# The squared-ReLU MLP of layer 0 as seven products of halves, with the modulation and bias rows between its steps

## The chip, the cores and the metric

The program runs on one core of a Trainium2 chip. The core has five engines that matter here: PE (TensorE, matrix products), DVE (VectorE), ACT (ScalarE), POOL (GpSimd) and SP (SyncE, which here issues most DMAs). Each takes its instructions in order; between engines semaphores order the work. The metric is the device time of one launch in microseconds (us).

## The reference

Two encoder layers on x of 1024 rows and 1024 columns, in float32. Layer 0 mixes with latent attention (`mla_mixer`), layer 1 with dilated window attention (`dilated_mixer`). The change is in the last line, and in where `mod` is computed:

```python
for i in range(2):
    mod = (silu(c) @ ada_w[i] + ada_b[i]).reshape(B, 6, 1024)
    shift1, scale1, gate1, shift2, scale2, gate2 = (mod[:, s, None, :] for s in range(6))
    h = rms_norm(x, norm_mix[i]) * (1 + scale1) + shift1
    x = x + gate1 * (mla_mixer if i == 0 else dilated_mixer)(h, ...)
    h = rms_norm(x, norm_mlp[i]) * (1 + scale2) + shift2
    x = x + gate2 * (square(relu(h @ mlp_w1[i])) @ mlp_w2[i])      # 1024 -> 4096 -> 1024
```

## The kernel before

**Products.** Every float32 product is made of three: `split` writes an operand as a high part (ACT) and a low part (DVE's subtraction, line 117, or another engine's through `lo_eng`), and `mm3` (lines 387 to 389) does high × high, high × low and low × high into PSUM. A matmul here is 128x128 by 512 columns unless said otherwise.

**Layer 0's MLP** is `mlp` (line 919 on). It walks 16 chunks `c` of 256 hidden columns. `up` multiplies the weights of a chunk with h, transposed (`psu`, 48 matmuls a chunk and half of the rows), applies Relu on ACT, the square on DVE, and splits; `down` multiplies that with the chunk's 256 rows of `mlp_w2` (`psy`) and DVE adds the result to x in SBUF (`x<-x,psy`, line 960). All of x stays in SBUF.

**Fillers.** Between its steps `mlp` calls functions from the list `filler`: `ada_step`, `bias_even` once, and `write`. `ada_step` works off the modulation row of the coming layer: each call issues the load of the next 512 KB piece of `ada_w` (tile `adaw`, on SP, in program order) and does the sum of the piece loaded by the call before on DVE (`ada_sum`, line 171, tile `adacc`); after eight pieces `ada_end` adds the bias row and lets a few small matmuls (`psac`) sum over the partitions. `bias_even` builds the position bias tables of layer 1's attention, and each `write` sends a piece of them to DRAM (tile `bt` reads them later). The modulation rows of both layers are worked off in one list: (0, 2), (0, 4), (0, 3), (0, 5), then (1, 1), (1, 0), (1, 2), (1, 4), (1, 3), (1, 5), where the second number is s above. Three of the calls are made by layer 0's `proj_res`.

**Layer 1's MLP** is `mlp7` (line 1003 on), which computes both products as a two-by-two block product with seven block products in place of eight. In the up half each of 16 pairs of 128 hidden columns takes seven products `(L.., R..)` in the order of the list `order`, where L11, L12, L22, S1 to S4 are sums of quarters of the weights (`ws` by POOL, split into `wf`), and R11, R21, R22, T1 to T4 are sums of quarters of h, split once into `hf` by `h_forms`. One product is 12 matmuls (`psm<-hf,wf`). The results are summed, put through Relu and square (`square`), summed again (`u_sums`, tiles `us`) and stored to DRAM (`uf`, `u_store`). The down half goes product by product, each in eight steps `gr` of 24 matmuls (`psm<-dh,dl`): `d_load`, called two steps ahead, loads the u form (`ufr`) and the needed quarters of `mlp_w2` (`w2r`, up to three), `d_form`, one step ahead, makes the weight's form (`w2s`, `w2T`) and splits both; T2's step also keeps the forms of T3 and T2 in SBUF. At the end of a product its four PSUM tiles are combined, multiplied with the gate, added to a part of x (`fin`; x is loaded again from DRAM, `xm`) and stored. What is the same in both layers' tails is `h_steps`, which makes h for the next stage.

**Output projection.** `proj_res` multiplies the attention's result with `w_o`, adds to x, and runs the steps that make h between its products. With `forms=True` (layer 1) these are `h_forms`, and x is stored to `xm` by POOL's DMA queue.

**What sets the order.** The program is written in an order; a planner that estimates the duration of every instruction may move them within an engine's queue, but what is `pinned` keeps its place: all DMAs of `ada_step` and `write`. Tiles come from pools with a fixed number of buffers: `G` (29 large tiles), `T` (temporaries, four a tag), and `X` (the auxiliary pool, `aux(n)`), and a load waits until the buffer that it takes is free.

Of the kernel before, what the change touches and what calls it, by code (L numbers as in the profile page):

```python
# [41 lines left out]
class K:  # L42
# [11 lines left out]
    def aux(self, n=16, ada=True):  # L54
# [3 lines left out]
        if ada:  # L58
            self.dap = self.ax.enter_context(self.tc.tile_pool(name=self.nm("ada"), bufs=2, reuse_waits="tile"))
# [149 lines left out]
    def ada_end(self, l, s, acc, row, psp, tag):  # L209

        nc = self.nc
        PS = lambda: psp.tile([P, 512], F32, tag=tag, bufs={"m": 1, "t": 3, "h": 2}.get(tag), name=self.nm("psac"))
# [12 lines left out]
    def ada_step(self, psp, tag):  # L225
# [3 lines left out]
        if self.ada_todo:  # L229
            l, s, j = self.ada_todo.pop(0)  # L230
            w = None
            if j < 8 or s % 3 == 2:
                w = self.dap.tile([P, 1024], F32, tag="w", name=self.nm("adaw"))
# [8 lines left out]
        if cur:  # L242
            l, s, j, w = cur
            if j == 0:
                self.ada_acc = self.dap.tile([P, 1024], F32, tag="acc", bufs=1, name=self.nm("adacc"))
# [42 lines left out]
    def xT(self, xh, d, psp, tag):  # L288

        ps = psp.tile([P, 512], F32, tag=tag, bufs={"h": 2, "u": 3, "m": 8}.get(tag), name=self.nm("pst"))  # L290
        for i in range(4):
            self.nc.tensor.transpose(ps[:, i * P : (i + 1) * P], xh[i][:, d * P : (d + 1) * P], self.ident)
        return ps
# [38 lines left out]
    def h_forms(self, xs0, xs1, mods, xalloc):  # L332
# [4 lines left out]
        R, keep = {}, []  # L337
# [16 lines left out]

        def first(psp, tag, d):
# [7 lines left out]
        def second(psp, tag, d):  # L363
            x1, x2 = (self.xT(xh[1], e, psp, tag) for e in (d, d + 4))
            t1, t4 = keep[d // 2][:, d % 2, :], keep[2 + d // 2][:, d % 2, :]
            r, t2 = xalloc("hs", (P, 2, 512), F32), self.T("ht2")
            t3, r22 = r[:, 0], r[:, 1]
            tt = lambda eng, o, x, y: eng.tensor_tensor(o, x, y, op=ALU.subtract)
# [13 lines left out]
        steps[1] += [lambda psp, tag, d=d: second(psp, tag, d) for d in range(4)]  # L382
        return (R, steps[0]), (R, steps[1])
# [483 lines left out]
    def proj_res(self, O, order, wo, gate, xs, mods, xalloc, ada, forms=False, done=None):  # L867
# [4 lines left out]
        with self.tc.tile_pool(name="psO", bufs=6, space=PSUM, reuse_waits="tile") as psp:  # L872
# [18 lines left out]
            if forms:  # L891
                (at, steps), (at1, steps1) = self.h_forms(xs[0:4], xs[4:8], mods, xalloc)
            else:
                at, steps = self.h_steps(xs[0:4], mods, xalloc, single=True)
                at1, steps1 = self.h_steps(xs[4:8], mods, xalloc, single=True)
            for i in range(8 + 6):
                if i < ada:
                    self.ada_step(psp, "h")
# [3 lines left out]
                if i >= 6:  # L902
                    part(pss[i - 6], *items[i - 6], 6, 8)
                    finish(pss[i - 6], *items[i - 6])
                    if items[i - 6][1] == 1:
                        steps.pop(0)(psp, "h")
                        if done:
                            done(items[i - 6][0])
            for i, (t, b) in enumerate(items):
# [3 lines left out]
                if b == 1:  # L913
                    steps1.pop(0)(psp, "h")
                    if done:
                        done(t + 4)
# [5 lines left out]
    def mlp(self, l, at0, second, gate, xs, filler, done, nxt=None):  # L922


        nc, a = self.nc, self.a
        NC = FF // 256
        with self.tc.tile_pool(name="psM", bufs=2, space=PSUM, reuse_waits="tile") as psp:

            def w1(c):
                return [self.wsplit(a["mlp_w1"][l, g * 512 : (g + 1) * 512, c * 256 : (c + 1) * 256]  # L930
                                    .rearrange("(d p) f -> p d f", p=P), (P, 4, 256), "w1") for g in range(2)]

            def w2(c):
                return [self.wsplit(a["mlp_w2"][l, (2 * c + f) * P : (2 * c + f + 1) * P, :], (P, 1024), "w2", row=gate)
                        for f in range(2)]

            def up(w, us, half, f):
                if f == len(us):
                    us.append([self.X(f"u{k}") for k in range(2)])
# [1040 lines left out]
```

## Time and profile before

| | |
|---|---|
| median of 3 runs | 3572.96 us (3566.36 to 3573.47) |
| profiled execution | 3570.81 us, span 3569.0 us, granted clock 0.983 |
| output projection, layer 0 | 741 to 835 us |
| MLP of layer 0 | 836.0 (first `psu`) to 1575.2 (last `psy`) |
| first matmul of layer 1's attention | 1580.3 |
| output projection, layer 1 | 2830 to 2922 |
| MLP of layer 1, up half | 2922.3 (first `psm`) to 3255.7 |
| MLP of layer 1, down half | 3256.9 to 3563.2 (last `psm`) |

Times of the stages are microseconds from the start of the span of the profiled execution. In the rows of the profile, `out<-in` names tiles without their numbers, `xN` counts instructions, a bracket or the part behind the last bar tells how long the engine sat idle before them and what ended that. PE and PEld are the matmuls and the weight loads of TensorE, PEclk is the clock that was granted to it as a share of full speed.

### The profile page before, as it was taken

How to read it: one execution, taken by the hardware profiler on the slowest of the kernel's cores; microseconds unless marked ns; L12 is line 12 of the kernel's file. 1: busy time of each engine (PE TensorE's matmuls, PEld its weight loads, DVE VectorE, ACT ScalarE, POOL GpSimd, SP SyncE). 2: the span in 40 equal slices, each digit the busy share in tenths (PEclk: the TensorE clock that was granted, in tenths of full speed). 3: DMA queues.
4: the chain of work that ended last, by engine and by line, in shares of the span. 5: the costliest groups of instructions: out<-in, count | busy, mean ns of one | idle time of the engine just before them, and what ended most of it. 6: DMA issues, size and time to landing. Idle time of an engine off the chain costs nothing.

```text
span 3569.0 us, 58220 instructions
## 1 busy us (share of the span) xinstructions
PE 3405.2 (95%) x21734; PEld 3036.5 (85%) x21734; DVE 2420.1 (68%) x4536; ACT 1573.2 (44%) x3279; POOL 1142.0 (32%) x1503
## 2 busy tenths in 40 slices
PE   6989989999999999999999999999999798999999
PEld 6878878878777888889999999999999676888887
DVE  6777877857555654566666666675787659776667
ACT  5557767633111222235555555564555334333432
POOL 6454444420011111112222222232333317653144
PEclk9999999999999999999999999999999898999999
DMA  5442222332444431123233333332333723446765
GB/s 183 136 160 71 101 68 69 113 118 90 106 106 107 112 95 48 60 91 93 80 107 107 103 100 103 98 88 68 107 104 99 192 86 121 157 151 240 275 227 165
DMA packets 341355, 419.99 MB, mean 118 GB/s; under 512 B 28901, under 2 KB 254482, under 8 KB 341066
## 3 DMA queue, kind: packets, MB, share of 16 engines
q1 hardware_dynamic: 331946, 394.11, 35.7%
q0 software_dynamic: 9120, 22.09, 1.9%
q8 instruction: 174, 2.85, 0.3%
q14 instruction: 115, 0.94, 0.1%
HBM read 319.35 MB, written 85.24 MB: 113 GB/s over the span
## 4 chain that ended last, share of the span: by engine, by line
PE 82%; DVE 6%; ACT 3%; DMA 3%; issue 2%; POOL 2%; SPq 0%; DVEq 0%; POOLq 0%; ACTq 0%
PE psproj L387 8%; PE psproj L389 8%; PE psproj L388 8%; PE psm L388 5%; PE psm L389 5%; PE psm L387 5%; PE psy L387 5%; PE psy L389 4%; PE psy L388 4%; PE psu L387 3%; PE psu L389 3%; PE psu L388 3%; PE pav L808 2%; PE pss L1590 2%; DMA adaw<-in_ada_w 2%
## 5 line engine op out<-in xcount | busy, mean ns | idle before, releaser
L404 POOL TENSOR_TENSOR w2r<-w2r,gate 128x1024 f32<-128x1024 f32 x32 | 84.7, 2648 | 677.4 <-DMA w2r<-in_mlp_w 664.1
L387 PE MATMUL psproj<-wqkh,hTp 128*128 128x256 f32 x1024 | 296.8, 290 | 0.0
L389 PE MATMUL psproj<-wqkh,hTp 128*128 128x256 f32 x1024 | 291.5, 285 | 0.0
L388 PE MATMUL psproj<-wqkl,hTp 128*128 128x256 f32 x1024 | 289.9, 283 | 0.0
L960 DVE TENSOR_TENSOR x<-x,psy 128x1024 f32<-128x1024 f32 x128 | 155.6, 1217 | 143.4 <-PE psy L389 143.4
L784 POOL TENSOR_SCALAR p<-p,arl 128x1024 f32<-128x1024 f32 x128 | 144.1, 1126 | 267.7 <-DVE arl L783 215.6
L1544 POOL TENSOR_TENSOR qn<-qn,dgain 128x128 f32<-128x128 f32 x192 | 90.1, 491 | 403.7 <-DVE qn L1541 373.9
L387 PE MATMUL psy<-w2h,u 128*128 128x512 f32 x512 | 203.1, 397 | 12.9 <-DVE x L960 12.9
L388 PE MATMUL psy<-w2l,u 128*128 128x512 f32 x512 | 202.0, 395 | 0.0
L389 PE MATMUL psy<-w2h,u 128*128 128x512 f32 x512 | 201.7, 394 | 0.0
L387 PE MATMUL psu<-hT,w1h 128*128 128x512 f32 x512 | 200.1, 391 | 0.9 <-DVE ht L315 0.9
L389 PE MATMUL psu<-hT,w1l 128*128 128x512 f32 x512 | 199.4, 390 | 0.0
L388 PE MATMUL psu<-hT,w1h 128*128 128x512 f32 x512 | 199.3, 389 | 0.0
L388 PEld LDWEIGHTS psproj<-wqkl,hTp 128*128 128x128 f32 x1024 | 195.8, 191 | 0.0
L389 PEld LDWEIGHTS psproj<-wqkh,hTp 128*128 128x128 f32 x1024 | 195.6, 191 | 0.0
L387 PEld LDWEIGHTS psproj<-wqkh,hTp 128*128 128x128 f32 x1024 | 195.6, 191 | 0.0
L1601 ACT ACTIVATE pd<-pd,dnb 128x192 f32<-128x192 f32 (+2 forms) x384 | 168.5, 443 | 54.8 <-DVE dnb L1599 54.6
L387 PE MATMUL psm<-hf,wf 128*128 128x512 f32 x448 | 177.1, 398 | 10.7 <-ACT wf L116 10.7
L389 PE MATMUL psm<-hf,wf 128*128 128x512 f32 x448 | 177.5, 397 | 5.6 <-DVE wf L117 5.6
L388 PE MATMUL psm<-hf,wf 128*128 128x512 f32 x448 | 177.7, 397 | 1.8 <-DVE hf L117 1.7
L1619 DVE TENSOR_TENSOR pT<-pspt,pT 128x512 f16<-128x512 f32 (+1 forms) x192 | 114.6, 598 | 94.8 <-ACT pT L1618 94.6
L117 DVE TENSOR_TENSOR pT<-ppt,pT 128x512 fp32r<-128x512 f32 x256 | 167.2, 681 | 14.1 <-ACT pT L116 13.3
(383 smaller groups left out, 11146.4 us busy)
## 6 DMA issues: line engine op xcount, KB each, us to landing
w2r<-in_mlp_w SPq DMA_DIRECT2D x104, 512.0 KB, 5.3
adaw<-in_ada_w SPq DMA_DIRECT2D x96, 512.0 KB, 5.8
w1r<-in_mlp_w SPq DMA_DIRECT2D x64, 512.0 KB, 4.1
bt<-bias SPq DMA_DIRECT2D x128, 256.0 KB, 3.2
ufr<-uf SPq DMA_DIRECT2D x56, 512.0 KB, 3.6
wqkr<-in_dil_w_in SPq DMA_DIRECT2D x96, 256.0 KB, 4.2
qkv<-st SPq DMA_DIRECT2D x32, 512.0 KB, 2.9
hraw<-qkv SPq DMA_DIRECT2D x32, 512.0 KB, 4.8
```

What stands on the lines that cost most here:

```text
L117: (lo_eng or nc.vector).tensor_tensor(lo, src, hi.bitcast(F32), op=ALU.subtract)
L387: mm(out, lh, rh, start=first, stop=False)
L388: mm(out, lh, rl, start=False, stop=False)
L389: mm(out, ll, rh, start=False, stop=last)
L404: nc.gpsimd.tensor_tensor(raw, raw, row, op=ALU.mult)
L784: nc.gpsimd.tensor_scalar(p, p, rl, 1.0, op0=ALU.mult, op1=ALU.mult)
L808: nc.tensor.matmul(ps[:, j % 2, :], heads[h]["v"][:, kt, :], u["pT"][hl][kt // 4][:, kt % 4, :], start=kt == 0 and hl == 0, stop=kt == 7 a ...
L960: nc.vector.tensor_tensor(xs[t], xs[t], ps, op=ALU.add)
L1544: nc.gpsimd.tensor_tensor(qq[:, i], qq[:, i], gain[:, g : g + 1, :].broadcast_to([P, 2, 64]), op=ALU.mult)
L1590: nc.tensor.matmul(ps[:, e * 256 : (e + 1) * 256], q[:, e, k, :], u["k"][:, e, w0 : w0 + 256], start=k == 0, stop=k == 1)
L1601: nc.scalar.activation(p[:, e, lo:hi], p[:, e, lo:hi], AF.Exp, bias=nb[:, e : e + 1], accum_out=stat[g][:, t, 1, 2 * pr + e : 2 * pr + e + 1])
L1619: nc.vector.tensor_tensor(pT[:, 1, 0 : 2 * n * P], ps[:, 0 : 2 * n * P], pT[:, 0, 0 : 2 * n * P], op=ALU.subtract)
```

## The change

`mlp` is gone; `mlp7` now serves both layers. What else is different:

- **Layer 0's output projection** runs `h_forms`, stores x to `xm[0]`, and makes no `ada_step`.
- **`h_forms`**: the four steps `second` make the sums and only the form T2; the forms of T3, T1, T4 and R22 are made afterwards, one kind a step (`others`). R22's low half moves from POOL to DVE.
- **Order of the seven**: up half R11, T2, R21, T3, T1, T4, R22 with the weights' forms made for pairs 0 and 1 together at the start; down half R11, T2, R21, T1, R22, T3, T4. The up half keeps its order; in the down half T1 and R22 come before T3 and T4, so the last part of x to be finished is that of rows 512 to 1023, columns 0 to 511.
- **Squares**: Relu and Square both on ACT (before: the square, or both, on POOL or DVE). `u_sums` uses one tile less.
- **In layer 0** the low half of the u forms for R11, R21, R22 and T3 is made by POOL (`lo_eng`); `ada_step` is called once a pair for pairs 2 to 14 (at k = 4) and, from the list `more`, in the steps 0 to 7 and from 16 on of the down half; `bias_even` is in step 1, a `write` in every second step from 6. The last product of the down half is interleaved with the first half of `h_steps` of layer 1. x goes to `xd` through POOL's queue, except the last four stores, which go through SP's.
- **Modulation row (1, 5)** moves to layer 1: one `ada_step` in each of the first 11 steps of its down half.
- **Pools**: `aux` has 19 buffers in layer 0 (16, beside a pool of three for `ada_step`) and 20 in layer 1, and `ada_step` takes its tiles from it.

```diff
         def second(psp, tag, d):
...
             tt(nc.vector, t1, t3, t1)
             tt(nc.vector, t2, r22, t1)
             form("T2", d, t2)
             tt(nc.gpsimd, t3, r22, t3)
-            form("T3", d, t3)
             tt(nc.gpsimd, t4, t4, t2)
-            form("T1", d, t1)
-            form("T4", d, t4)
-            form("R22", d, r22, nc.gpsimd)
+
+        def others(name):
+            src = {"T3": [r[0] for r in rs], "T1": keep[0:2], "T4": keep[2:4], "R22": [r[1] for r in rs]}[name]
+            for d in range(4):
+                form(name, d, src[d // 2][:, d % 2, :])
 
         steps[0] += [lambda psp, tag, d=d: first(psp, tag, d) for d in range(8)]
...
-            if forms:
-                (at, steps), (at1, steps1) = self.h_forms(xs[0:4], xs[4:8], mods, xalloc)
-            else:
-                at, steps = self.h_steps(xs[0:4], mods, xalloc, single=True)
-                at1, steps1 = self.h_steps(xs[4:8], mods, xalloc, single=True)
+            (at, steps), (at1, steps1) = self.h_forms(xs[0:4], xs[4:8], mods, xalloc)
             for i in range(8 + 6):
-                if i < ada:
-                    self.ada_step(psp, "h")
...
-        UF = {n: i for i, n in enumerate(("L11", "L12", "L22", "S1", "S2", "S3", "S4"))}
-
-        order = [("L11", "R11"), ("S2", "T2"), ("L12", "R21"), ("S3", "T3"), ("S1", "T1"), ("L22", "T4"), ("S4", "R22")]
+        UF = {n: i for i, n in enumerate(("L11", "S1", "L12", "L22", "S3", "S2", "S4"))}
+
+        prod = [("L11", "R11"), ("L12", "R21"), ("S4", "R22"), ("L22", "T4"), ("S1", "T1"), ("S2", "T2"), ("S3", "T3")]
+        order, order2 = ([prod[i - 1] for i in o] for o in ((1, 6, 2, 7, 5, 4, 3), (1, 6, 2, 5, 3, 7, 4)))
...
-                def square(eng, o, x, y):
+                def square(o, x, y):
 
                     tt(nc.vector, o, x, y)
-                    if eng is nc.vector:
-                        eng.scalar_tensor_tensor(o, o, 0.0, o, op0=ALU.max, op1=ALU.mult)
-                    else:
-                        nc.scalar.activation(o, o, AF.Relu)
-                        tt(eng, o, o, o, ALU.mult)
+                    nc.scalar.activation(o, o, AF.Relu)
+                    nc.scalar.activation(o, o, AF.Square)
...
             def u_sums(u):
-                u.s = [self.X("us", (P, 2, 512), F32) for _ in range(2)]
-                tt(nc.vector, u.s[0][:, 0], u.a[:, 1], u.b[:, 1])
-                tt(nc.vector, u.s[0][:, 1], u.s[0][:, 0], u.a[:, 0], ALU.subtract)
-                tt(nc.gpsimd, u.s[1][:, 0], u.a[:, 0], u.a[:, 1], ALU.subtract)
-                tt(nc.gpsimd, u.s[1][:, 1], u.b[:, 0], u.s[0][:, 1], ALU.subtract)
+                u.s, u.s4 = self.X("us", (P, 2, 512), F32), self.T("us4")
+                (u11, u12), (u21, u22), (s3, s2) = ((x[:, 0], x[:, 1]) for x in (u.a, u.b, u.s))
+                tt(nc.gpsimd, s3, u11, u12, ALU.subtract)
+                tt(nc.vector, u12, u12, u22)
+                tt(nc.vector, s2, u12, u11, ALU.subtract)
+                tt(nc.gpsimd, u.s4, u21, s2, ALU.subtract)
...
-                    self.split(hi, lo, x)
+                    self.split(hi, lo, x, lo_eng if x is u and rn in ("R11", "R21", "R22", "T3") else None)
...
+            for c in range(2):
+                quarters(c)
+            for n in ("L11", "L12"):
+                for c in range(2):
+                    u_forms(c, (n,))
+            for f in ((0, 0), (1, 0), None, (0, 2), None, (1, 2), None, None):
+                if f:
+                    up(us[f[0]], f[1])
+                else:
+                    steps.pop(0)(psp, "m")
+            for c in range(2):
+                sums(c)
+                u_forms(c, ("S2",))
+            todo = (1, 3, 4, 5, 6)
+            for j, i in enumerate(todo):
+                up(us[0], i)
+                if steps:
+                    steps.pop(0)(psp, "m")
+                if j < 4:
+                    for c in range(2):
+                        u_forms(c, (names[todo[j + 1]],))
+                up(us[1], i)
+                if j == 1:
+                    raws[2] = w_load(2)
+                elif j == 2:
+                    quarters(2)
+                    u_forms(2, names[0:1])
+                elif j == 3:
+                    sums(2)
+                    u_forms(2, names[1:3])
+                elif j == 4:
+                    raws[3] = w_load(3)
+                    u_forms(2, names[3:7])
             ld, fm = {}, {}
             dsteps = [(i, g) for i in range(7) for g in range(NP // 2)]
-            for c in range(NP):
-                todo = [1, 3, 4, 5, 6] if c < 2 else list(range(7))
-                if c == 0:
-                    u_forms(0, ("S3",))
...
+            for c in range(2, NP):
+                for k in range(7):
+                    if c == 2 and k in (0, 2):
+                        (u_sums(us[0]) if k == 0 else u_store(us[0], 0))
...
+                        u_sums(us[c - 1])
+                    elif k == 3:
+                        u_store(us[c - 1], c - 1)
+                    elif k == 4 and l == 0 and c + 1 < NP:
+                        self.ada_step(psp, "m")
+                    up(us[c], k)
...
+            more = list(more)
+            h = None
             c1, c2 = slice(0, 512), slice(512, 1024)
             for n, (i, gr) in enumerate(dsteps):
+                for f in more.pop(0) if more else ():
+                    f(psp, "m")
                 if n + 2 <= last:
...
                 if gr == 0:
                     ps = [M() for _ in range(4)]
-                    if i in (1, 3):
+                    if i == 2:
+                        g = self.gate(l, 1)
+                    if i in (1, 4):
                         x_load(0 if i == 1 else 4)
                     if i == 6:
                         for t in range(4):
                             z = self.T("z")
-                            tt(nc.gpsimd, z, at(U4, t), g[:, c2], ALU.mult)
-                            tt(nc.gpsimd, xs[t][:, c2], xs[t][:, c2], z)
+                            tt(nc.gpsimd, z, at(U3, t), g[:, c1], ALU.mult)
+                            tt(nc.gpsimd, xs[t + 4][:, c1], xs[t + 4][:, c1], z)
+                        if nxt is not None:
+                            h, hsteps = self.h_steps(xs[0:4], nxt)
+                            hsteps.pop(0)(psp, "m")
+                if h is not None:
+                    hsteps.pop(0)(psp, "m")
...
         k.bias_any()
-        k.aux()
+        k.aux(19)
         mctx = ExitStack()
         k.mp = mctx.enter_context(tc.tile_pool(name="mla", bufs=1))
-        k.ada_start([(0, s) for s in (2, 4, 3, 5)] + [(1, s) for s in (1, 0, 2, 4, 3, 5)])
...
-        at, second = k.proj_res(O, (4, 5, 0, 1, 2, 3, 6, 7), wo, gate, xs, mods(0, 3), k.X, 3)
+        xm = [k.dp.tile([S, D], F32, name=f"xm{l}") for l in range(2)]
+        keep_x = lambda l: (lambda t: nc.gpsimd.dma_start(out=xm[l][t * P : (t + 1) * P, :], in_=xs[t]))
+        forms, (_, steps) = k.proj_res(O, (4, 5, 0, 1, 2, 3, 6, 7), wo, gate, xs, mods(0, 3), k.X, done=keep_x(0))
         xd = k.dp.tile([S, D], F32, name="xd")
+        k.ada_start([(1, s) for s in (1, 0, 2, 4, 3)])
...
 
-            fill = [[k.ada_step] for _ in range(56)]
-            fill[0].append(lambda psp, tag: writes.extend(k.bias_even(bp, psp, tag)))
-            for f in fill[6::3]:
+            fill = [[k.ada_step] if n < 8 or n >= 16 else [] for n in range(54)]
+            fill[1].append(lambda psp, tag: writes.extend(k.bias_even(bp, psp, tag)))
+            for f in fill[6::2]:
                 f.append(write)
-            at = k.mlp(0, at, second, k.gate(0, 1), xs, fill,
-                       lambda t: nc.gpsimd.dma_start(out=xd[t * P : (t + 1) * P, :], in_=xs[t]), mods(1, 0))
+            xs, at = k.mlp7(0, forms, steps, xm[0],
+                            lambda t, c, x, eng: eng.dma_start(out=xd[t * P : (t + 1) * P, c], in_=x[:, c]),
...
 
-        k.mlp7(1, forms, steps, xm, store)
+        k.ada_start([(1, 5)])
+        k.mlp7(1, forms, steps, xm[1], store, [[k.ada_step]] * 11)
         k.aux_end()
 
```

More of the change, by code (lines that the diff above doesn't have):

```diff
@@ L1005, in mlp7 @@
-    def mlp7(self, l, R, steps, xd, out):
+    def mlp7(self, l, R, steps, xd, out, more=(), lo_eng=None, nxt=None):
         nc, a = self.nc, self.a
@@ L1107, in d_form @@
             def d_form(i, g, ld):
-                rn = order[i][1]
+                rn = order2[i][1]
                 u, q = ld
@@ L1155, in mlp7, with sums @@
-            u_forms(0, ("S2",))
-            while steps:
-                steps.pop(0)(psp, "m")
-            names = [o[0] for o in order]
+            def sums(c):
+                w_sums(us[c].L, us[c].q)
+            for c in range(2):
[8 more added lines that the diff above has]
+                    steps.pop(0)(psp, "m")
@@ L1925, in program @@
                 nc.sync.dma_start(out=xs[t][p0 : p0 + n, :], in_=s)
-        xm = k.dp.tile([S, D], F32, name="xm")
-        forms, (_, steps) = k.proj_res(O, range(8), wo, got["gate"], xs, mods(1, 3), k.X, 0, forms=True,
-            done=lambda t: nc.gpsimd.dma_start(out=xm[t * P : (t + 1) * P, :], in_=xs[t]))
+        forms, (_, steps) = k.proj_res(O, range(8), wo, got["gate"], xs, mods(1, 3), k.X, done=keep_x(1))
         def store(t, c, x, eng):
```

200 lines of the change are left out of this document (54 added, 146 removed).

## The prediction, made before the changed kernel was run

> **What bounds the kernel now.** I read the page first (engines, then the chain), then the windows stage by stage, then tiles and waits inside the two MLPs.
>
> ```profile
> span 3569.0 us, 58220 instructions
> PE 3405.2 (95%) x21734; PEld 3036.5 (85%) x21734; DVE 2420.1 (68%) x4536; ACT 1573.2 (44%) x3279; POOL 1142.0 (32%) x1503
> PE 82%; DVE 6%; ACT 3%; DMA 3%; issue 2%; POOL 2%; SPq 0%; DVEq 0%; POOLq 0%; ACTq 0%
> ```
>
> PE carries 82% of the chain, so a matmul that disappears is worth its spacing as long as nothing else becomes late. The windows give busy time, instruction count, granted clock and DMA share of each stage: the output projection of layer 0, the two halves of its MLP (up to 1262, then to 1576), the output projection of layer 1, and its seven-product MLP cut into start-up, up half, down half, and the last two products of the down half.
>
> ```profile
> core 0: us, PE busy (x) PEld busy (x) DVE busy (x) ACT busy (x) POOL busy (x), PEclk, DMA share, GB/s
> 741.00:835.00 94.00, 91.65 (x422) 75.40 (x422) 51.69 (x89) 25.00 (x46) 6.82 (x8) 1.00 0.38 124
> 835.00:1262.00 427.00, 413.16 (x1823) 337.62 (x1822) 255.51 (x267) 91.37 (x127) 47.77 (x18) 0.98 0.40 105
> 1262.00:1576.00 314.00, 313.54 (x1401) 257.98 (x1400) 176.46 (x172) 66.11 (x94) 40.73 (x21) 1.00 0.21 65
> 2830.00:2922.00 92.00, 88.47 (x407) 73.22 (x405) 44.51 (x89) 20.29 (x44) 4.40 (x8) 0.99 0.37 111
> 2922.00:2975.00 53.00, 38.47 (x135) 26.91 (x136) 40.89 (x42) 26.57 (x47) 35.03 (x23) 0.72 0.14 46
> 2975.00:3256.40 281.40, 281.40 (x1243) 233.01 (x1242) 216.88 (x272) 86.96 (x145) 166.25 (x116) 1.00 0.44 154
> 3256.40:3569.00 312.60, 305.44 (x1345) 251.85 (x1343) 213.13 (x166) 113.94 (x112) 107.20 (x70) 0.99 0.70 240
> 3474.40:3518.00 43.60, 42.86 (x189) 35.16 (x189) 37.46 (x29) 16.23 (x16) 23.93 (x17) 1.00 0.66 218
> 3518.00:3561.60 43.60, 43.60 (x194) 36.10 (x193) 34.55 (x23) 10.39 (x10) 22.07 (x20) 1.00 0.45 131
> ```
>
> In the up half of layer 1, PE never rests: 281.40 us for 1243 matmuls, 0.2264 us each. That is the price of a matmul below. Seven-product code thus runs at the full rate once it is going; it loses in the start-up (clock 0.72, 53 us) and comes near its limits in the down half (DMA 0.70).
>
> **The change part by part.** The profiled execution took 3570.8 us (span 3569.0), 2.2 under the median of 3573.0; the sum is made against 3570.8.
>
> *A. Fewer matmuls.* The tiles of both MLPs, with first and last start:
>
> ```profile
> L387 PE MATMUL psu<-hT,w1h x512: 388/389/501, 836.0 to 1527.6; 128*128 128x512 f32 x171
> L389 PE MATMUL psy<-w2h,u x512: 388/389/632, 885.3 to 1575.2; 128*128 128x512 f32 x171
> L387 PE MATMUL psm<-hf,wf x448: 387/389/794, 2922.3 to 3255.7; 128*128 128x512 f32 x150
> L389 PE MATMUL psm<-dh,dl x448: 388/389/397, 3256.9 to 3563.2; 128*128 128x512 f32 x150
> ```
>
> Three lines of 512 per half make 3072 matmuls in layer 0, three of 448 make 2688 in layer 1; the built order of the changed program has 384 PE instructions fewer. 384 × 0.2264 = **−87**.
>
> *B. Waits of layer 0's old MLP that go.* 1262 to 1576 has no idle PE: 314/1401 = 0.2241 a matmul, short ones included. At that rate the 1823 of the stage before need 408.6 of its 427 us: 18.4 lost.
>
> ```profile
> DVE adacc L171 <- DMA adaw<-in_ada_w: 42.8, 17, 6.0
> ```
>
> DVE stood 42.8 us, 17 times, at the sums of the modulation rows, which it takes in order ahead of the copies that PE needs. A few of the stage's short matmuls are shorter than the mean, so I take **−20** (18 to 25).
>
> *C. Start-up of the seven products, now also in layer 0.*
>
> ```profile
> L292 PE MATMUL pst<-ident,xh 128*128 128x128 f32 x32 | 3.8, 272 | 0.0
> L117 DVE TENSOR_TENSOR hf<-hk,hf 128x512 fp32r<-128x512 f32 x8 | 9.9, 1243 | 0.0
> L117 DVE TENSOR_TENSOR hf<-hs,hf 128x512 fp32r<-128x512 f32 x4 | 2.7, 679 | 0.0
> L368 POOL TENSOR_TENSOR hs<-hs 128x512 f32<-128x512 f32 x4 | 7.0, 1739 | 9.8 <-DVE hk L368 9.8
> 2949.71 1.58 DVE L368 TENSOR_TENSOR ht<-hs,hk 128x512 f32<-128x512 f32 x1
> 2949.01 1.73 POOL L368 TENSOR_TENSOR hk<-hk,ht 128x512 f32<-128x512 f32 x1
> ```
>
> Of the 135 PE instructions in 2922 to 2975, 32 are transposes of a quarter of the columns: (103 + 32/4) × 0.2264 = 25.1 of useful time in 53, so 28 lost. DVE sets it: beside a POOL operation its 512-column operation takes 1.58 us where alone it takes 0.68. The new order (pairs 0 and 1 together, the other forms of h after T2) puts about 33 DVE operations ahead of the second S2 form, 16 of them beside POOL: 16 × 1.7 + 17 × 0.68 = 38.8 after some 12 us, so 51; then nine products of 12 matmuls (24.5) and 2.5 of cold clock: 78 us, where the present order reaches the same 168 matmuls at 53 + (168 − 103) × 0.2264 = 67.7. That is +10 with every pair taken at its slowest; I take +6 for the new order (−8 to +14), so **+34** for layer 0.
>
> *D. Layer 0's down half with the modulation and bias steps in it.*
>
> ```profile
> GB/s 285 317 309 294 343 358 387 406 388 387 107 233 380 389 359 360 365 372 399 412 415 391 387 386 386 388 353 401 379 385 390 363 384 398 369 384 385 406 373 393
> DMA packets 15803, 32.05 MB, mean 364 GB/s; under 512 B 970, under 2 KB 970, under 8 KB 15798
> q1 hardware_dynamic: 15798, 31.99, 99.6%
> w2r<-in_mlp_w SPq DMA_DIRECT2D x34, 512.0 KB, 6.6
> L117 DVE TENSOR_TENSOR dl<-ufr,dh 128x1024 fp32r<-128x1024 f32 x55 | 87.4, 1590 | 46.7 <-ACT dh L116 27.8 <-POOL w2s L1011 18.4
> ```
>
> That is the DMA view of 3256 to 3344, the first two products: full for 88 us, 364 GB/s, or 1.44 us for 512 KB. Seven modulation loads and five bias writes join there: 12 × 1.44 = 17.3, less the dip to 107 and 233; I take +15 (4 to 23). The T1 product now comes fourth, with three weight loads, a modulation load and half a write a step: 4.5 × 1.44 = 6.5 against 24 × 0.2264 = 5.43 on PE, eight steps, 8.5; +7 (0 to 12). In the last product DVE has the 37.46 us of the row 3474 to 3518 (T4's forms) plus the next layer's first h steps inserted there:
>
> ```profile
> L315 DVE TENSOR_SCALAR ht<-pst,mod,mod x36: 800/804/809, 72.5 to 1615.8; 128x512 f32<-128x512 f32 x36
> L264 DVE TENSOR_SCALAR xh<-x,xry 128x1024 f32<-128x1024 f32 x1 | 0.8, 753 | 0.0
> ```
>
> 8 × (0.80 + 0.68) + 4 × 0.75 = 14.8, together 52.3 against 43.6 of PE: 8.7, and the POOL burst of 3518 (22.07 us) slows DVE as in C; +11 (0 to 20). Together **+33**. By the Trainium skill, "DMA: Bandwidth & Descriptors", section "Where 436 GB/s comes from", the limit of the memory is about 358 GB/s a core: the twelve transfers would be 17.6. The trace's slices reach 415 GB/s, so the measured mean is used.
>
> Else the two halves are taken as layer 1 shows them, the storing and reloading of the u forms included. Nothing is charged for the up half of layer 0, where each pair gets one 1.39 us modulation sum and its load: DVE is busy 216.9 of 281.4 us and DMA 0.44. If that cover were gone, 13 × 1.39 = 18 would come back. Nor for the squares, now all on ACT (87 of 281), nor for the gate row of layer 1, which only moves between layers.
>
> *E. End of layer 0.*
>
> ```profile
> 1570.22 0.93 SPq L1480 DMA_DIRECT2D wvr<-in_dil_w_in  x2
> 1580.24 1.23 DVE L117 TENSOR_TENSOR wvl<-wvr,wvh 128x1024 fp32r<-128x1024 f32 x1 [2.84 <-ACT wvh L116]
> ```
>
> The attention's first weights are asked for 5 us before the old MLP's last matmul. Afterwards they stand on SP behind the last four stores of x, which wait for the very last matmuls: **+4** (0 to 6).
>
> *F. Layer 1.* It gets the new start-up (+6), eight modulation loads in the full stretch (8 × 1.44 = 11.5, some into the dip: +8, 0 to 11.5), and T4 as last product, whose POOL form joins the final POOL burst:
>
> ```profile
> L1011 POOL TENSOR_TENSOR w2s<-w2r,w2T 128x1024 f32<-128x1024 f32 x8 | 21.3, 2664 | 10.8 <-PE psm L388 10.8
> ```
>
> 21.3 + 22.07 = 43.4 us of POOL in 43.6 of PE: +5 (0 to 10). Together **+19**.
>
> *G. Output projection of layer 0* loses its three modulation steps and becomes layer 1's, whose eight stores of x go out on a POOL that is busy 4.4 us of 92: 92 for 94, **−2**.
>
> −87 − 20 + 34 + 33 + 4 + 19 − 2 = −19: 3552; I say **3550**, bounds of the terms combined about 3520 to 3575.
>
> **The rivals.** *Fast:* the added stalls don't come, since loads are asked for two steps ahead and the dips absorb them; layer 0 then costs only layer 1's start-up: 3570.8 − 87 − 20 + 28 − 2 = 3490. For it: layer 1's down half, with DMA at 99.6%, still gives PE 305.44 of 312.60. Against: there the transfers just fit, with nothing added. Chance 0.17.
>
> *Port:* DVE and POOL slow each other throughout layer 0's down half, because the low halves of four u forms (32 operations) go to POOL.
>
> ```profile
> L1011 POOL TENSOR_TENSOR w2s<-w2r,w2r 128x1024 f32<-128x1024 f32 x8 | 19.3, 2413 | 39.1 <-PE psm L389 20.1 <-DMA w2r<-in_mlp_w 13.0 <-DVE dl L117 6.0
> L1011 DVE TENSOR_TENSOR w2T<-w2T,w2r 128x1024 f32<-128x1024 f32 x8 | 9.7, 1218 | 5.0 <-POOL w2T L1011 5.0
> L171 DVE SCALAR_TENSOR_TENSOR adacc<-adaw,cond,adacc 128x1024 f32<-128x1024 f32 x38 | 52.9, 1391 | 46.6 <-DMA adaw<-in_ada_w 46.3
> ```
>
> In turns: POOL 56 × 2.41 + 20 halves of 1.2 = 159; DVE 80 splits at 1.23, 8 × 1.22, 28 sums at 1.39, 12 × 0.68 = 155. 314 exceeds 1344 × 0.2264 = 304 by 10: 3560. For it: the pairs of C; against: the C pair overlaps a little (1.73 and 1.58 against alone-times that add to more), and only part of the 28 sums fall beside POOL. Chance 0.15. The Trainium skill, "SBUF — State Buffer", section "Who interferes with whom", states it as a lock: a DVE instruction with two inputs in SBUF contends with a GpSimd instruction reading SBUF and the loser waits; the rows agree (1243 ns mean against 679).
>
> *Slower:* the wait of B moves into the seven products. Some 28 sums of modulation rows stand in order on DVE ahead of each step's splits; a load there takes 6.6 us median to land, longer than a step of 5.43. Before, 20 us of PE were lost over 17 waits, 1.2 each; at 28 that is 33, added to the forecast's terms: 3585. It decides once a load lands later than the step it was asked a step ahead for. Against it: DVE has 99 us free of 312. Chance 0.20.
>
> That the change doesn't do what it says is excluded by the built order.
>
> **How the numbers follow.** The forecast has 0.48. 0.2% (7 us) is about what a measurement of this kernel can tell from no change. Faster: 0.43 of the forecast, the fast rival's 0.17, 0.12 of the port's: 0.72. Same: 0.05 + 0.02. Slower: 0.20 + 0.01. The range 3495 to 3590 leaves out the fast rival's half and the slow one's tail.
>
> **What would show it.** 2688 matmuls in layer 0's stage; its start-up with some 34 us lost and a clock about 0.7; its down half longer than 313 us with DMA near full in the first two products (D), DVE full in the last; idle at adacc only if the slow rival holds; dil's first matmul up to 9 us behind the last psm. The forecast is wrong if layer 0's MLP takes under 665 us or over 735 (741 before).

## The result: slower, 3601.8 us for 3573.2

The changed kernel takes 3601.84 us (median of 4 runs, 3594.45 to 3607.3) where the kernel before takes 3573.22: a ratio of 1.0083, 95% interval 1.006 to 1.0105. The prediction was 3550, range 3495 to 3590: wrong, and on the wrong side. The profiled execution took 3600.57 us.

The page of the changed kernel, span, engines and chain:

```profile
span 3598.8 us, 58602 instructions
PE 3346.6 (93%) x21350; PEld 2977.7 (83%) x21350; DVE 2449.7 (68%) x4588; ACT 1759.0 (49%) x3575; POOL 1336.1 (37%) x1627
PE 75%; DVE 7%; ACT 4%; DMA 3%; issue 3%; POOL 2%; SPq 0%; POOLq 0%; DVEq 0%; ACTq 0%
```

There are 384 matmuls fewer (21350 for 21734) and PE is busy 59 us less, yet the span is 30 us longer: PE stands idle, and its share of the chain fell from 82% to 75%. Where, the windows of layer 0's output projection and MLP tell (start-up, up half, then the seven products of the down half in their order, with the boundary T3 to T4 cut out):

```profile
core 0: us, PE busy (x) PEld busy (x) DVE busy (x) ACT busy (x) POOL busy (x), PEclk, DMA share, GB/s
755.00:851.00 96.00, 91.56 (x418) 75.00 (x416) 45.57 (x88) 23.43 (x47) 10.26 (x14) 1.00 0.37 126
851.00:910.00 59.00, 40.40 (x153) 30.78 (x154) 45.05 (x52) 27.25 (x49) 30.46 (x20) 0.77 0.08 25
910.00:1189.00 279.00, 279.00 (x1241) 231.39 (x1240) 191.57 (x253) 137.94 (x237) 119.33 (x83) 1.00 0.53 178
1189.00:1245.00 56.00, 50.91 (x221) 41.08 (x220) 35.71 (x37) 19.05 (x20) 23.82 (x10) 0.91 0.93 301
1245.00:1307.00 62.00, 49.84 (x191) 36.40 (x190) 29.39 (x27) 18.99 (x21) 23.36 (x9) 0.94 1.03 321
1307.00:1353.00 46.00, 46.00 (x199) 36.40 (x197) 26.96 (x18) 14.45 (x14) 19.59 (x8) 1.00 1.03 319
1353.00:1414.00 61.00, 50.65 (x208) 40.38 (x208) 49.12 (x38) 19.05 (x19) 32.05 (x17) 0.92 1.00 328
1414.00:1459.00 45.00, 45.00 (x206) 37.45 (x204) 29.03 (x21) 19.52 (x19) 23.02 (x10) 1.00 0.82 287
1459.00:1503.50 44.50, 44.47 (x199) 36.59 (x199) 33.36 (x22) 17.67 (x21) 30.58 (x16) 1.00 0.50 166
1503.50:1528.30 24.80, 0.15 (x2) 0.16 (x2) 24.70 (x18) 4.21 (x8) 21.29 (x17) 0.60 0.31 106
1528.30:1577.50 49.20, 49.20 (x224) 40.37 (x224) 30.92 (x33) 16.46 (x22) 10.03 (x4) 0.96 0.19 66
```

A product is 192 matmuls, 43.5 us at 0.2264. The up half runs at that rate once started. In the down half R11, T2 and T1 take 56 to 62 us with DMA full and the rate at 301 to 328 GB/s, and between T3 and T4 PE does next to nothing for 24.8 us. A full queue alone is not the loss: R21 has the same DMA share and rate (1.03, 319 GB/s), and PE never rests in it. The first and last starts of the tiles, layer 0 above, layer 1 below (answers cut to the two MLPs), give the stages:

```profile
L389 PE MATMUL psm<-hf,wf x448: 387/389/796, 851.7 to 1188.5; 128*128 128x512 f32 x150
L391 PE MATMUL psm<-dh,dl x448: 387/389/628, 1189.6 to 1577.3; 128*128 128x512 f32 x150
L389 PE MATMUL psm<-hf,wf x448: 387/389/796, 2928.8 to 3265.3; 128*128 128x512 f32 x150
L391 PE MATMUL psm<-dh,dl x448: 388/389/632, 3266.4 to 3591.6; 128*128 128x512 f32 x150
```

| stage, us (profiled executions) | before | after | difference | forecast |
|---|---|---|---|---|
| start to the output projection of layer 0 | 742.0 | 755.0 | +13.0 | 0 |
| that projection | 94.0 | 96.7 | +2.7 | −2 |
| MLP of layer 0 | 739.4 | 725.6 | −13.8 | −40 |
| to the attention's first matmul | 4.9 | 9.6 | +4.7 | +4 |
| attention and projection of layer 1 | 1342.0 | 1341.9 | 0 | 0 |
| MLP of layer 1, up half | 334.1 | 337.1 | +3.0 | +6 |
| its down half | 307.0 | 325.7 | +18.7 | +13 |
| end | 5.6 | 7.2 | +1.6 | 0 |

Three things were missed: 13 us at the very start, 26 in layer 0's MLP, 6 in layer 1's down half. PE's waits in layer 0's down half (engine, line, waited for, us, times, longest) show the largest one, and the row of the old MLP beside it what its waits had really cost PE. The third row is the attention's first matmul, behind the MLP:

```profile
PE pst L290 <- DVE xh L283: 24.7, 1, 24.7
PE psm L389 <- ACT dh L114: 13.2, 9, 4.2
PE psproj L389 <- ACT wvh L114: 9.2, 1, 9.2
PE psm L390 <- DVE dl L115: 9.2, 5, 4.3
PE psb L1299 <- DVE oh L1266: 4.9, 2, 3.7
```

```profile
PE psy L387 <- DVE x L960: 12.9, 4, 5.0
```

### The profile page after: what moved, and what is told of

It reads as the page before. It is cut to its first block, busy times and chain, and to the rows that moved or that the text cites. A ratio compares the mean times of both kernels' runs of the same rounds, so it can differ in the third digit from the quotient of the medians.

```text
span 3598.8 us, 58602 instructions
## 1 busy us (share of the span) xinstructions
PE 3346.6 (93%) x21350; PEld 2977.7 (83%) x21350; DVE 2449.7 (68%) x4588; ACT 1759.0 (49%) x3575; POOL 1336.1 (37%) x1627
## 4 chain that ended last, share of the span: by engine, by line
PE 75%; DVE 7%; ACT 4%; DMA 3%; issue 3%; POOL 2%; SPq 0%; POOLq 0%; DVEq 0%; ACTq 0%
PE psm L391 10%; PE psm L390 10%; PE psm L389 10%; PE psproj L389 7%; PE psproj L391 7%; PE psproj L390 7%; PE pav L810 3%; PE pss L1537 2%; PE ppt L797 2%; PE pspt L1563 2%; DMA w2r<-in_mlp_w 2%; PE psq L1506 2%; PE psy L391 2%; PE psy L390 2%; PE psy L389 2%
## 5 line engine op out<-in xcount | busy, mean ns | idle before, releaser
L389 PE MATMUL psm<-hf,wf 128*128 128x512 f32 x896 | 356.0, 397 | 24.3 <-ACT wf L114 24.3
L391 PE MATMUL psm<-hf,wf 128*128 128x512 f32 x896 | 353.2, 397 | 21.3 <-DVE wf L115 21.3
L390 PE MATMUL psm<-dl,dh 128*128 128x512 f32 x896 | 357.8, 399 | 15.4 <-DVE dl L115 15.0
L391 PE MATMUL psm<-dh,dl 128*128 128x512 f32 x896 | 355.2, 396 | 0.0
L390 PE MATMUL psm<-hf,wf 128*128 128x512 f32 x896 | 354.2, 395 | 0.0
L389 PE MATMUL psm<-dh,dh 128*128 128x512 f32 x896 | 333.7, 399 | 19.5 <-ACT dh L114 19.5
L114 ACT ACTIVATE dh<-ufr 128x1024 fp32r<-128x1024 f32 x112 | 118.4, 1057 | 253.1 <-DMA ufr<-uf 79.4
L389 PEld LDWEIGHTS psm<-hf,wf 128*128 128x128 f32 x896 | 172.0, 192 | 62.4 <-ACT wf L114 27.5
L390 PEld LDWEIGHTS psm<-dl,dh 128*128 128x128 f32 x896 | 172.5, 193 | 59.6 <-DVE dl L115 23.1
L391 PEld LDWEIGHTS psm<-hf,wf 128*128 128x128 f32 x896 | 171.4, 191 | 60.8 <-DVE wf L115 25.1
L389 PEld LDWEIGHTS psm<-dh,dh 128*128 128x128 f32 x896 | 170.5, 192 | 61.7 <-ACT dh L114 24.9
L391 PEld LDWEIGHTS psm<-dh,dl 128*128 128x128 f32 x896 | 172.2, 192 | 35.9
L390 PEld LDWEIGHTS psm<-hf,wf 128*128 128x128 f32 x896 | 171.8, 192 | 35.9
```

Source lines behind the costliest of these rows:

```text
L114: nc.scalar.activation(hi, src, AF.Copy)
L389: mm(out, lh, rh, start=first, stop=False)
L390: mm(out, lh, rl, start=False, stop=False)
L391: mm(out, ll, rh, start=False, stop=last)
```

## The experiments

Every variant starts from the changed kernel. Lengths of the products of layer 0's down half, each from its first matmul to that of the next, and of the up half, in us from the traces; the last column is the median with the ratio to runs of the kernel before on the same chip. Gains are told from the ratios, times 3573 us, since the kernel before itself differs by up to 3 us between chips. The interval of the changed kernel alone is 8 us to either side, so a gain under some 10 us is not clear of noise; there the lengths of the products, each of one profiled execution, carry the argument:

| kernel | up | R11 | T2 | R21 | T1 | R22 | T3 | T4 | time |
|---|---|---|---|---|---|---|---|---|---|
| changed | 337.4 | 55.5 | 62.8 | 46.0 | 60.9 | 45.2 | 68.6 | 49.0 | 3601.8, 1.0083 [1.006, 1.0105] |
| e1_aux18 | 340.2 | 55.5 | 63.6 | 45.9 | 63.1 | 45.2 | 61.4 | 49.4 | 3586.1, 1.0045 [1.0029, 1.0061] |
| e2_lead | 337.9 | 55.6 | 63.6 | 46.2 | 59.7 | 45.7 | 43.7 | 58.3 | 3582.6, 1.0042 [1.0026, 1.0058] |
| e3_ada_up | 352.3 | 48.7 | 59.6 | 45.4 | 49.3 | 43.5 | 67.3 | 49.4 | 3588.6, 1.0055 [1.0038, 1.0072] |
| e4_bias_up | 365.8 | 57.5 | 50.2 | 45.9 | 48.5 | 45.2 | 68.7 | 49.7 | 3606.7, 1.0105 [1.0088, 1.0122] |
| e5_writes | 337.4 | 55.5 | 49.9 | 45.6 | 49.4 | 57.2 | 69.6 | 49.8 | 3587.5, 1.0046 [1.003, 1.0062] |
| e6_lo | 337.9 | 53.5 | 61.4 | 45.6 | 61.0 | 45.2 | 68.6 | 49.3 | 3595.1, 1.0067 [1.0043, 1.009] |
| e11_act | 337.4 | 55.5 | 65.9 | 46.2 | 60.5 | 45.2 | 60.8 | 49.7 | 3596.0, 1.007 [1.0052, 1.0088] |
| e7_mix | 342.1 | 51.3 | 48.6 | 45.9 | 54.8 | 53.7 | 52.4 | 65.7 | 3579.0, 1.0022 [1.0011, 1.0033] |
| e8_mix1 | 341.5 | 48.7 | 48.0 | 45.9 | 50.4 | 58.1 | 53.5 | 65.1 | 3565.4, 0.9978 [0.9965, 0.9991] |
| e9_act | 339.3 | 48.9 | 50.6 | 45.9 | 54.5 | 53.9 | 52.3 | 61.5 | 3561.8, 0.9977 [0.9965, 0.9988] |
| e10_late | 341.5 | 48.9 | 51.4 | 45.9 | 54.2 | 45.4 | 46.9 | 68.7 | 3554.1, 0.9956 [0.9943, 0.9969] |

**The start: which buffer a tile gets.**

```diff
-        k.aux(19)
+        k.aux(18)
```

> The changed kernel with 18 buffers in layer 0's auxiliary pool in place of 19. The 13th tile taken from the pool then lies beside, not on, the memory that the skipped branch of the bias tables would have used for its stored tiles, so the first squares of x on ACT no longer wait for all DMA queues. Theory (slot): ACT's first xh starts near 11 us as before the change, not at 22.3, the latent attention's first score product near 223 us, not 236.6, and the kernel takes 10 to 14 us less than the changed one. Rival (the delay comes from SP's own loads, which stand behind eight 512 KB issues): no change in the first 260 us, total the same within 3 us.

ACT's first square of x in the kernel before, in the changed one, and with 18 buffers (start, duration, and in brackets the idle time before it and what ended it):

```profile
11.30 1.06 ACT L274 ACTIVATE xh<-x 128x1024 f32<-128x1024 f32 x1 [8.70 <-DVEq L1376]
```

```profile
22.31 1.06 ACT L272 ACTIVATE xh<-x 128x1024 f32<-128x1024 f32 x1 [19.66 <-SPq L1323]
```

```profile
12.03 1.06 ACT L272 ACTIVATE xh<-x 128x1024 f32<-128x1024 f32 x1 [9.42 <-PEq L1323]
```

That the number of buffers does it is shown: it moves this instruction by 10.3 us, the kernel gains 14, and the attention's first score product comes at 222.4 us, not 236.6 (222.6 before the change). In all seven profiled variants with 19 buffers that product comes at 235 to 237 us, in all five with 18 at 222 to 226. Why is read from the program, and no trace shows it. Buffers are handed out from the top of the pool downward, so the number of buffers decides on what memory the 13th tile falls. With 19 it is that of tiles which the branch for irregular positions would store by DMA; the branch isn't taken, but the program makes the tile's first user wait for every DMA queue, and SP goes through its part of that only at 22 us (L1323 in the row above is the branch).

**The next layer's h: no lead.**

```diff
-                if h is not None:
+                for _ in range((0, 0, 0, 0, 2, 2, 2, 2)[gr] if h is not None else 0):
                     hsteps.pop(0)(psp, "m")
```

> The changed kernel with the transposes of the next layer's h two a step in the last four steps of layer 0's last product (T4), where the changed kernel has one a step from the first step on, right behind the statistics of x. Theory (no lead): the 24.7 us in which PE waits for xh goes; DVE still has some 55 us of work in that product, so T4 with the step before it shrinks from 74 to 54 to 58 us and the kernel takes 15 to 20 us less. Rival (DVE and POOL's work sets the product's length wherever the transposes stand): the wait reappears at the splits of T4, total within 5 us of the changed one.

T3 and T4 together fall from 117.6 to 102.0 us, and the kernel gains 15, the lower end of what was expected. The transposes stood on PE right behind the statistics of x, ahead of everything else of T4. In the old MLP the products of two row tiles stood between the two. That DVE's work then shows (T4 58.3) is as expected; a wait of 7.7 us for `xh` is still in it.

**Why the wait was so long.** DVE and POOL of the changed kernel in that gap:

```profile
1517.88 1.19 DVE L109 SCALAR_TENSOR_TENSOR xry<-xrt,xry 128x4 f32<-128x4 f32 x1
1519.10 10.98 DVE L283 TENSOR_SCALAR xh<-x,xry 128x1024 f32<-128x1024 f32 x4
```

```profile
1519.59 1.27 POOL L925 TENSOR_TENSOR z<-du,gate 128x512 f32<-128x512 f32 x1
1520.81 1.27 POOL L925 TENSOR_TENSOR x<-x,z 128x512 f32<-128x512 f32 x1
1522.02 0.58 POOL L1854 DMA_DIRECT2D xd<-x  x1
1522.61 1.27 POOL L925 TENSOR_TENSOR z<-du,gate 128x512 f32<-128x512 f32 x1
1523.84 3.69 POOL L925 TENSOR_TENSOR x<-x,z 128x512 f32<-128x512 f32 x3
```

Of the 10.98 us of four operations the first alone has 8.99 (the other three 0.74 each): it ends 0.6 us after POOL's row of operations, whose end is at 1527.5.

```diff
-                            h, hsteps = self.h_steps(xs[0:4], nxt)
+                            h, hsteps = self.h_steps(xs[0:4], nxt, act=True)   # x times its scale on ACT, not DVE
```

> The changed kernel with one thing else: the normalised x of the next layer's first h steps is made by ACT, four operations of about 1.05 us, in place of DVE, whose first one took 8.99 us, until POOL had finished six operations in a row; the transposes stand where the changed kernel has them. Theory (DVE is shut out while POOL works): the wait of PE ahead of the first transpose falls from 24.7 to 15 to 18 us, the kernel takes 7 to 9 us less than the changed one. Rival (the statistics of x, ready at 1519, set the wait, and the shut-out was beside it): the wait falls by under 3 us.

```profile
PE pst L290 <- ACT xh L281: 16.8, 1, 16.8
```

The wait falls by 7.9 us, inside the expected range; the kernel gains 5, less than expected and within the noise (T2 was 3 us longer in the profiled run). The other 16.8 are the statistics, queued on DVE behind the evictions of T3.

**The modulation rows.**

```diff
-                    elif k == 4 and l == 0 and c + 1 < NP:
+                    if k in (1, 3, 5) and l == 0 and c + 1 < NP:
...
-            fill = [[k.ada_step] if n < 8 or n >= 16 else [] for n in range(54)]
+            fill = [[k.ada_step] if 16 <= n < 25 else [] for n in range(54)]
```

> The changed kernel with the modulation steps of layer 0 moved: three a pair in the up half (39), nine in the third product of the down half (R21, one weight load a step), none elsewhere in the down half. Theory (fillers): R11 falls from 55.5 to about 49 us, T2 from 62.8 to about 58, T1 from 60.9 to about 48, the up half stays within 3 us of 337; total 20 to 26 us less than the changed kernel. Rival (the seven products' own loads fill the DMA queue, whatever stands beside): R11, T2 and T1 shrink by under 3 us each, total under 8 us less. Rival (the wait of DVE for modulation rows moves with them): the up half grows by 10 us or more.

```profile
PE psac L220 <- DVE adacc L169: 3.5, 2, 1.8
```

R11, T2 and T1 give 21.6 us, as the first theory has it, and the up half takes 14.9 of them back. That is the second rival's number, but mostly not its reason: the waits for the sums, in the row above, are 3.5 us. The rest fits PE's own work that moved along, the small matmuls `psac` that end each row: 36 more of them stand in the up half, 11.6 us by their durations, and 16 each (4 us) left R11 and T1. So of T1's 11.6 us at most some 8 are the loads'. The kernel gains 10. Two steps a pair cost the up half 2 to 5 us (the mixes).

**The bias tables and their writes.**

```diff
-            fill[1].append(lambda psp, tag: writes.extend(k.bias_even(bp, psp, tag)))
-            for f in fill[6::2]:
-                f.append(write)
+            mid = {(4, 0): [lambda psp, tag: writes.extend(k.bias_even(bp, psp, tag))]}      # up half, pair 4
+            mid.update({(c, j): [write] for c in range(6, 14) for j in (2, 6)})
```

> The changed kernel with the bias tables of layer 1 computed in the up half of layer 0 (pair 4, two tiles from the auxiliary pool) and their 16 writes at two a pair from pair 6 on, none in the down half. Theory (fillers): R11 falls from 55.5 to about 47 us (no PE wait of 4.9 us for the one-hot rows, no writes), T2 from 62.8 to about 56, T1 from 60.9 to about 57, up half within 3 us of 337; total 14 to 20 us less than the changed kernel. Rival (writes are as cheap as their bytes, 1.44 us for 512 KB): total 6 us less or under.

T2 and T1 shrink by 12.5 each, more than expected, but R11 grows by 2, the up half by 28, and the kernel loses 8: a miss in total. In the up half PE waits for the one-hot rows of the tables, 12.8 of the 28 us; the rest was not taken apart:

```profile
PE psb L1301 <- DVE oh L1268: 12.8, 3, 8.8
```

So the writes alone were moved:

```diff
-            for f in fill[6::2]:
+            for f in fill[32:48]:
```

> The changed kernel with the 16 bias writes alone moved: one in each of the steps 32 to 47 of layer 0's down half (products R22 and T3) in place of every second step from 6 on; the tables are still computed in step 1, the modulation steps stand where the changed kernel has them. Theory (the writes overfill the queue): T2 falls from 62.8 to 50 to 53 us and T1 from 60.9 to 49 to 52, as in the run with the bias work in the up half, R22 and T3 grow by under 4; total 16 to 22 us less than the changed kernel. Rival (it was the computation of the tables, which that run moved too): T2 and T1 stay above 58.

T2 falls to 49.9 and T1 to 49.4, as expected, but R22 grows by 12, which was not: a write a step is too many there. The kernel gains 13, less than expected. The DMA view of T2, first in the changed kernel (1244.7 to 1307.4 us), then in this one (1243.4 to 1293.3):

```profile
DMA packets 10915, 20.07 MB, mean 320 GB/s; under 512 B 614, under 2 KB 2929, under 8 KB 10912
q1 hardware_dynamic: 10912, 20.04, 103.3%
bias<-bv SPq DMA_DIRECT2D x4, 514.0 KB
```

```profile
DMA packets 8273, 17.44 MB, mean 349 GB/s; under 512 B 541, under 2 KB 541, under 8 KB 8270
```

The stage with the four writes moves 2.6 MB more and takes 12.9 us longer: 204 GB/s for what is added, 2.6 us a write at that rate where the prediction had 1.44. The packets between 512 bytes and 2 KB are theirs: rows of 257 floats, 1028 bytes. The packets' own times say nearly the same. In T2 of the changed kernel one of 1028 bytes takes 75 ns in the mean and one of 2048 bytes 101, so a write of 512 packets holds all 16 DMA engines for 2.4 us. The Trainium skill ("DMA: Bandwidth & Descriptors", section "Specifications") has 512 bytes as the smallest transfer at full rate; the packets here are twice that size, yet move 13.7 bytes a nanosecond on their engine where the 2048-byte ones move 20.2, so the measurement decides.

**The shared port.** The low halves of u go back to DVE (`lo_eng` None in layer 0).

> The changed kernel with the low halves of all u forms of layer 0 on DVE again, none on POOL. Theory (DMA and order set the down half): within 5 us of the changed kernel either way. Rival (port: DVE and POOL slow each other there): R21, R22 and T3, which run with DMA below its limit, don't change, and R11 and T2 shrink by 5 us or more in sum, since POOL's 2.4 us operations go.

R11 and T2 together give 3.4 us, R21, R22 and T3 nothing to speak of, the kernel 6, within the noise. So POOL's share of the splits is not what sets the down half.

**Together.** The slot, the lead, the writes in R22 and T3, modulation steps two a pair in the up half and none beside R11, T2 and T1:

> 18 buffers, the transposes two a step in the last four steps, the writes in steps 32 to 47, and the modulation steps two a pair in the up half (26) and one a step in steps 16 to 23 and from 32 on, none beside R11, T2 and T1. Theory (four separate places): the gains add: 14 for the start, 16 to 19 for the transposes, 7 of R11, 12 of T2, 12 to 14 of T1, less 5 to 8 in the up half: 53 to 60 us less than the changed kernel, so 3542 to 3549, which is 0.6 to 0.8% below the kernel before. Rival (one bound behind all of them, DVE and POOL together): 30 us less at most, not below the kernel before by 0.2%.

Only 22 of the 53 to 60 us came. T2 and the start behave about as in the single runs, R11 and T1 are 2.6 and 5.5 us longer than in e3_ada_up. R22 and T3 grow with the modulation rows and writes that are now put there; T4 is 7 us longer than in e2_lead, though nothing new is put into it. The rival's bound, 30 us at most, fits the total. Its reason, DVE and POOL together, has a part in T1 and T4, as the trace of the last version shows further down.

```diff
-        k.mlp7(1, forms, steps, xm[1], store, [[k.ada_step]] * 11)
+        k.mlp7(1, forms, steps, xm[1], store)            # and one ada_step a pair in layer 1's up half
```

> As the mix, and the modulation row of layer 1 in its own up half, one step a pair from pair 2 on, in place of the first eleven steps of its down half. Theory: layer 1's R11 falls from 50.5 to 45 us and T2 from 49 to 44, the up half stays at 337; 10 to 12 us less than the mix. Rival (the new order and the x loads cost there, not the modulation row): under 4 us less.

Layer 1's up half and its products R11 and T2 in this run:

```profile
2904.40:3243.60 339.20, 319.17 (x1380) 260.62 (x1381) 226.61 (x294) 164.34 (x283) 142.42 (x102) 0.96 0.42 144
3243.60:3288.20 44.60, 43.86 (x194) 35.96 (x193) 25.83 (x22) 20.89 (x22) 11.47 (x5) 1.00 0.99 356
3288.20:3331.70 43.50, 43.50 (x193) 36.03 (x192) 32.15 (x24) 18.48 (x20) 13.82 (x6) 1.00 0.99 366
```

44.6 and 43.5 us, for 50.4 and 49.0: the queue is still full, PE no longer waits. So the modulation row was the whole of that loss (its loads and DVE's sums moved together). Two more steps followed, the second starting from the first:

> As the mix with layer 1's row in its up half, and the normalised x of the next layer's first h steps made by ACT (four operations of about 1.05 us) in place of DVE, where they took 2.7 us each beside POOL. Theory (DVE's queue holds up the splits of T4): layer 0's T4 falls from 65 to 55 to 58 us; 6 to 10 us less. Rival (POOL's form for T4 and its gate products set it): under 3 us less.

> As the run before it in this job, with the 16 bias writes in the steps 40 to 53 (products T3 and T4, DMA share 0.5 and 0.2 in the changed kernel) in place of 32 to 47. At 2.6 to 2.9 us of all 16 DMA engines a write, T3 and T4 have room for them. Theory: R22 falls from 58 to 46 to 50 us, T3 stays within 3, the attention's start is up to 3 us later behind the last writes: 5 to 9 us less. Rival (R22's length comes from the modulation rows there, not from the writes): under 3 us less.

In e9_act T4 falls by 3.6 us, half of what was expected, and the ratio is that of e8_mix1: no gain that can be told. e10_late, on the same chip, is 7.6 us faster at the median: R22 is back at 45.4 and T3 at 46.9, T4 grows to 68.7. It is the version that beats both kernels, by 0.4% the one before (interval 0.3 to 0.6%). Its T4 is 25 us over the time of its matmuls, and PE waits there mostly for two low halves on DVE:

```profile
PE psm L390 <- DVE dl L115: 14.7, 2, 9.7
1489.41 7.49 DVE L115 TENSOR_TENSOR dl<-w2s,dh 128x1024 fp32r<-128x1024 f32 x1
1506.47 7.17 DVE L115 TENSOR_TENSOR dl<-w2s,dh 128x1024 fp32r<-128x1024 f32 x1 [5.28 <-ACT dh L114]
```

Such an operation takes 1.22 us by itself. Each of these two runs beside a row of POOL operations without a break (1489.2 to 1495.8 and 1505.4 to 1512.6) and ends some 1.1 us behind it: what delayed the first `xh` of the changed kernel. In T1 the same operation takes 5.74 us in e7_mix, e9_act and e10_late, where T1 is 54 to 55 us long; in e8_mix1 it does not, and T1 has 50.4. No run takes POOL out of these places, so there the cause is read from the rows and not tested.

## Why the prediction was wrong, by its steps

- **A, 384 matmuls fewer, −87:** right. 2688 matmuls do the work, and the up half ran them at 0.2264. That PE's busy time fell by 59 us only goes with the lower clock wherever it pauses (PEclk 0.91 to 0.94 in R11, T2 and T1); it was not taken apart.
- **B, waits that go, −20:** too high by some 6. PE's busy time was 413.16 us of the 427, so it stood idle for 14, 12.9 of them on x; DVE's 42.8 us for modulation rows mostly had cover. The remainder of the 18.4 is short matmuls or the lower clock (0.98 in that stage). No run takes this term alone.
- **C, start-up, +34 in layer 0:** about right: 337.4 − 1344 × 0.2264 = 33.1, of which some 4 are the small matmuls of a modulation row, which the old MLP had too. In layer 1 the new order cost 3.0 in place of 6.
- **D, the down half, +33:** the step that failed. It takes 388.1 us, 84 over its 1344 matmuls. Some 25 of these are short matmuls, which the old MLP had as well, so about 59 stand against the 33. R11 and T2 lose 31 (forecast 15), T1 17 (7), T3 and T4 31 (11), in which 7, 4 and 9 us of short matmuls are counted too. Two of its terms were mis-sized for one reason each. A bias write was priced by its bytes at the mean rate of large loads; it costs 2.4 to 2.6 us (e5). And the last product was counted as a sum of DVE's work against PE's time, 8.7 us over, without asking what stands ahead of what on PE: PE was made to wait for a chain that had only begun (e2), lengthened by POOL (e11). With its 725.6 us the MLP stays inside the 665 to 735 that the prediction gave as its sign, near the upper end; what carried the total out of the range is D together with the start.
- **E, +4:** right, 4.7.
- **F, layer 1, +19:** 23.3 (3.0, 18.7 and 1.6); the modulation row cost 11 to 12 us (e8), the upper bound given, not 8. T4 as the last product takes 52.2 us where the last product before took 43.3: 9, not 5, inside the range given.
- **G, −2:** +2.7, not explained by a run.
- **Not in the sum at all:** the start, +13. The change of the pool's size stands in the list of changes and has no term in the sum; on what memory the buffers fall was not asked (e1).
- **The rivals:** the slower one got the sign, not by its mechanism: DVE waits for modulation rows only 8.0 us in the down half, and the longest PE waits are for other things. Of its two ingredients the landing time matters (T1 gives 11.6 us when the loads leave with their small matmuls, e3), but T1 gives the same when the writes leave (e5). The two gains are not to be added: with both gone T1 takes 50.4 to 54.8 us (the mixes), at a DMA share of about 0.8, so what is left there is not a full queue. The fast rival was far off. The port rival is small as a throughput (e6) and large at single places, as a shut-out: tested in T3's end (e11), seen in T1 and T4 of the mixes.

## What to carry to other kernels

A step that is moved into another loop brings its order along: ask for each engine what stands directly behind it there, and give a chain over three engines a few steps' lead before PE needs its end. A stage in which PE waits on a full queue pays for every added transfer at that transfer's own rate, so price it by a slice of the trace in which such transfers run, not by the mean. After changing a pool's size, look at what the first instructions of each engine wait for. And look for DVE operations that take several times their usual length: what stands beside them on POOL is the next thing to move.

## What was not expected of the hardware

One DVE operation with one tensor input (x times a number per partition, 0.74 us by itself) took 8.99 us beside a run of POOL operations of 1.27 us and ended 0.6 us after the last of them. By its end it was not slowed but shut out, and not for one POOL operation but for six, the DMA issue between them included. The Trainium skill ("SBUF — State Buffer", section "Who interferes with whom") says that such an operation can take both port pairs and that the engine which comes second is blocked for the whole of the other's instruction; the trace agrees, and goes on: between POOL's back-to-back instructions DVE did not get in. Operations with two tensor inputs show the same (7.49 us for 1.22 in e10_late), and in e2_lead one on 128x4 numbers, 0.15 us elsewhere, took 11.72. It is not always so: in T1 of the changed kernel one of 1.22 us took 3.39 and ended while POOL's next operation was under way. What decides between the two was not found.
